# Value products of two units formed with 512 weight columns at a time, in one layer of a hybrid decoder

## The chip, the cores and the metric

The kernel runs on one core of a Trainium2 chip. The metric is the device time in microseconds (us) of that core; a time of the kernel is the median of its runs. TensorE multiplies matrices, VectorE and ScalarE work element by element, GpSimd does small jobs here, and SyncE's queue issues the transfers. A matrix product on TensorE is an instruction pair: a weight load brings the stationary operand into the array, and the matmul streams the moving operand through it into a PSUM bank. A bank holds 512 f32 values on each of 128 partitions.

## The reference, cut to what matters

```python
u = rmsnorm(h, norm_w[l])
proj = jnp.einsum('bsd,dc->bsc', u, w_in[l])            # 1024 tokens, 2048 -> 8200 columns
(ml_q, ml_k, ml_v, ml_o, ml_z, ml_i, ml_f,
 hg_q, hg_f, hg_i, hg_g) = jnp.split(proj, split_points, axis=-1)
qk = silu(causal_dwconv(concat([ml_q, ml_k]), conv_w[l], conv_b[l]))
h_a = mlstm_chunkwise(q_a, k_a, v_a, i_pre, f_pre)      # 4 heads, qk 128, value width 256
y_a = sigmoid(ml_o) * rmsnorm(h_a, ml_norm_w) * silu(ml_z)
h_b = hgrn2_chunkwise(hg_q, k_b, logf_b, hg_i)          # 8 heads, state 128 x 128
y_b = rmsnorm(h_b, hg_norm_w) * silu(hg_g)
h = h + einsum('bsc,cd->bsd', concat([y_a, y_b]), w_out[l])
gate = sigmoid(einsum('bsd,de->bse', rmsnorm(h, pe_norm_w[l]), w_pg[l]))
h = h + gate * einsum('bsr,rd->bsd', p[l], w_pe[l])
out = rmsnorm(h, final_norm_w)
```

The change concerns the two value columns sets, `ml_v` and `hg_i`: eight blocks of 256 columns, of which each product is (1024 x 2048) times (2048 x 256).

## The kernel before, in words

The 1024 tokens are worked on in two halves of 512. For each half the input is brought in transposed, 16 tiles `u` of 128 channels by 512 tokens, each as two parts (a rounded high part and the rest, low). Every weight is halved in the same way: `split` (L117) lets ScalarE write the high part (L118) and VectorE the rest (L119). A product then takes three matmuls, high by high, high by low, low by high (`mm3`, L245 to L248).

The combined projection is cut into 32 blocks `b` of 256 columns a half. Weights come as pieces of 512 KB, four for a block, in the order of the list `w_order` (L128 to L142). `next_piece` (L144) transfers one into `raw` and halves it into `hl`; both have three buffers, and a piece is asked for three pieces ahead (`AHEAD`).

Most blocks go through `proj_ch` (L250): the weights are stationary and the 512 tokens of the half move, into two PSUM banks `pj`. The value blocks go through `proj_tok` (L262): the activations are stationary, 128 tokens at a time, and the 256 weight columns move. Four banks `pt` are filled, one for each group of 128 tokens, and half of each is used. For a block that is 16 channels tiles x 4 token groups x 3 matmuls = 192 matmuls. The pool `pj` has four banks for both kinds.

A half has eight units, one after the other: four mLSTM heads (`mlstm_unit`, L345, blocks 4 hd to 4 hd + 3, the value block is the third) and four pairs of HGRN heads (`hgrn_unit`, L466, blocks 16 + 4 pr to 19 + 4 pr, the value block is the first). In the first head's value block eight gate columns ride along (264 columns). ScalarE reads the four banks of a value block into `vt` (L389, L476), scaled by each token's norm; `vt` has two buffers.

A unit's mixing follows its projections and runs beside the projections of the next unit: small products on TensorE with VectorE and ScalarE steps between them. For an HGRN unit I call this its chain. It starts with column sums (`cs_d`, `cs_s`, L518 and L519), goes through five levels (`pl`, L574, then a masked copy at L579 and two updates at L585 and L587), then states and outputs (`hkt`, `hpu`, `hpo`), a norm, and two transposes back (`hpt`, L644, then `hy`, L646). After both halves come the output projection (`po`), the gate projection (`pg`) and the last norm.

The order of the instructions on each engine is not the one in which the code is written. A scheduler places them from priorities and from its own costs when the program is built, so a change in one product moves the mixing steps between the products too. On the chip each engine then runs its list in that order and waits by semaphores.

Of the kernel before, what the change touches and what calls it, by code (L numbers as in the profile page):

```python
# [16 lines left out]
F32 = mybir.dt.float32  # L17
# [3 lines left out]
AF = mybir.ActivationFunctionType  # L21
# [3 lines left out]
P = 128  # L25
S = 1024
D = 2048
KT = D // P
HT = 512
NC = HT // P  # L30
# [4 lines left out]
BIG = 1e30  # L35
LEVELS = (4, 8, 16, 32, 64)
NMASK = 3 + len(LEVELS)
HOLD = 2
LATE = [f"bg1_3_{pc}" for pc in (1, 3, 5, 7)]

# [1 line left out]


@with_exitstack
def hybrid_layer(ctx: ExitStack, tc, x, xT, pT, w_blk, w_v0, w_out, w_pg, w_pe, vec, gb, fnw,
                 ident_in, causal_in, lmask_in, out):
    nc = tc.nc
    PS = bass.MemoryType.PSUM
# [14 lines left out]
    mix = mixctx.enter_context(tc.tile_pool(name="mix", bufs=1))  # L63

    def psj(name):
        return pj.tile([P, 512], F32, tag="pj", name=name)
# [10 lines left out]
    causal = const.tile([P, P], F32, name="causal")  # L77
    lmask = mix.tile([P, NMASK, 64], U32, name="lmask")
    gb_sb = const.tile([4, 2], F32, name="gb_sb")
# [48 lines left out]
    w_order, w_tiles = [], []  # L128
    for half in range(2):
        for b in range(32):  # L130
            for pc in range(4):
                src = w_v0 if b == 2 else w_blk[b]
                w_order.append((f"{half}_{b}_{pc}", src[:, pc * 4:(pc + 1) * 4, :]))
    for half in range(2):
# [31 lines left out]
    def load_piece(name):  # L166

        while len(w_tiles) < len(w_order) and (len(w_tiles) < AHEAD or w_order[len(w_tiles) - AHEAD][0] != name):
            next_piece()
        return dict(w_tiles[-AHEAD - 4:])[name]  # L170
# [74 lines left out]
    def mm3(ps, ah, al, bh, bl, first, last):  # L245
        nc.tensor.matmul(ps, lhsT=ah, rhs=bh, start=first, stop=False)  # L246
        nc.tensor.matmul(ps, lhsT=ah, rhs=bl, start=False, stop=False)  # L247
        nc.tensor.matmul(ps, lhsT=al, rhs=bh, start=False, stop=last)  # L248
# [13 lines left out]
    def proj_tok(half, us, b, n=256):  # L262

        ps = [psj(f"pt{half}_{b}_{i}") for i in range(NC)]
        for pc in range(4):
            hl = load_piece(f"{half}_{b}_{pc}")
            for kk in range(4):
                k = pc * 4 + kk
                sl = slice(kk * n, (kk + 1) * n)
                for t in range(NC):  # L270
                    ts = slice(t * P, (t + 1) * P)
                    mm3(ps[t][:, 0:n], us[k][:, 0, ts], us[k][:, 1, ts], hl[:, 0, sl], hl[:, 1, sl],
                        k == 0, k == KT - 1)
        return ps


    def gates(half, pv, rc):
# [68 lines left out]
    def mlstm_unit(half, us, hd, rs, gc):  # L346
        n = f"{half}_{hd}"
        b0 = hd * 4
# [4 lines left out]
        rc, rb = rs  # L353
# [22 lines left out]
        q, k = qk[:, 0], qk[:, 1]  # L376
# [5 lines left out]
            nc.vector.tensor_tensor(out=gate[:, i], in0=po[i], in1=rb, op=ALU.mult)  # L382
        nc.scalar.activation(out=gate, in_=gate, func=AF.Sigmoid)

        pv = proj_tok(half, us, b0 + 2, 264 if hd == 0 else 256)
        vt = mix.tile([P, NC, 257], F32, tag="vt", bufs=2, name=f"vt{n}")
        nc.vector.memset(vt[:, :, 256:257], 1.0)
        for t in range(NC):
            nc.scalar.activation(out=vt[:, t, 0:256], in_=pv[t][:, 0:256], func=AF.Copy, scale=rc[:, t:t + 1])  # L389
        if hd == 0:  # L390
            gc = gates(half, pv, rc)
        cols, rows = gc
# [75 lines left out]
    def hgrn_unit(half, us, pr, rs):  # L468
        rc, rb = rs
        b0 = 16 + pr * 4  # L470
        n = f"{half}_{pr}"
        H2 = 2 * NC
        pv = proj_tok(half, us, b0)
        vt = mix.tile([P, NC, 257], F32, tag="vt", bufs=2, name=f"hv{n}")
        for t in range(NC):
            nc.scalar.activation(out=vt[:, t, 0:256], in_=pv[t][:, 0:256], func=AF.Copy, scale=rc[:, t:t + 1])  # L476

        def v_of(i, c):
            return vt[:, c, i * P:(i + 1) * P]
# [3 lines left out]
        f = mix.tile([P, 2, HT + 3], F32, tag="raw", bufs=1, name=f"f{n}")  # L483
        f = f.rearrange("p a b -> p (a b)")[:, 0:2 * HT].rearrange("p (a b) -> p a b", b=HT)
        gate = mix.tile([P, 2, HT], F32, tag="gate", bufs=2, name=f"hgate{n}")
        for i in range(2):
            hd = pr * 2 + i
# [63 lines left out]
        for i in range(2):  # L551
            ps = col_sums(prod[:, i], f"s2{n}_{i}").rearrange("p (c b j t) -> p c b j t", c=NC, j=2, t=2)
            for j in range(2):
                nc.vector.copy_predicated(
                    out=at.rearrange("p c (b a s) -> p c b a s", a=2, s=2)[:, i * NC:(i + 1) * NC, :, 1, :],
# [11 lines left out]
        for li, s in enumerate(LEVELS):  # L567
# [10 lines left out]
            else:  # L578
                nc.vector.copy_predicated(  # L579
                    out=at.rearrange("p c (b two s) -> p c b two s", two=2, s=s)[0:M, :, :, 1, :],  # L580
# [15 lines left out]
        for i in range(2):  # L596
            hd = pr * 2 + i
# [40 lines left out]
        for i in range(2):  # L638
            hd = pr * 2 + i
# [12 lines left out]
    for half in range(2):  # L652
        us = prep_u(half)
        gc = None
        for hd in range(4):
            gc, rs = mlstm_unit(half, us, hd, rs, gc)
        nrs = prep_stats(1) if half == 0 else None
        if half == 1:
            mlctx.close()
            xh = ctx.enter_context(tc.tile_pool(name="xh", bufs=4, side="right", reuse_waits="tile"))  # L660
        for pr in range(4):
            hgrn_unit(half, us, pr, rs)
        rs = nrs
# [4 lines left out]
    for half in range(2):  # L668
# [14 lines left out]
        for cb in range(4):  # L683
            ps = [psj(f"po{half}_{cb}_{t}") for t in range(NC)]
            for pc in range(8):
                hl = load_piece(f"o{half}_{cb}_{pc}")
                for kk in range(2):
                    k = pc * 2 + kk
# [16 lines left out]
            for j in range(4):  # L705
                k = cb * 4 + j
# [15 lines left out]
        def gate_block(cb, ts_, pref):  # L722
# [13 lines left out]
            for t in ts_:  # L736
                parts = 2 if pref == "b" and t == NC - 1 else 1
                w = 512 // parts
                units += [(t, slice(i * w, (i + 1) * w), psj(f"pg{half}_{cb}_{t}_{i}")) for i in range(parts)]
            hold = HOLD if pref == "b" else 8  # L740
            hls = []
# [58 lines left out]
def _layout(inp):  # L800
    f = np.float32
    x = np.ascontiguousarray(np.asarray(inp["x"])[0])
    w = np.asarray(inp["w_in"])[0]
    cols = []
    for h in range(4):
        cols.append([(h * 128, 128), (512 + h * 128, 128)])
        cols.append([(2048 + h * 256, 256)])
        cols.append([(1024 + h * 256, 256)])
        cols.append([(3072 + h * 256, 256)])
    for p in range(4):  # L810
        q, fg, i, g = 4104 + p * 256, 5128 + p * 256, 6152 + p * 256, 7176 + p * 256
        cols.append([(i, 256)])
        cols.append([(q, 128), (fg, 128)])
        cols.append([(q + 128, 128), (fg + 128, 128)])
        cols.append([(g, 256)])
    v0 = np.empty((P, KT, 264), f)
    v0[:, :, 0:256] = w[:, 1024:1280].reshape(KT, P, 256).transpose(1, 0, 2)
    v0[:, :, 256:264] = w[:, 4096:4104].reshape(KT, P, 8).transpose(1, 0, 2)
    blk = np.empty((32, P, KT, 256), f)
    for b, cs in enumerate(cols):  # L820
        o = 0
        for c, n in cs:
            blk[b, :, :, o:o + n] = w[:, c:c + n].reshape(KT, P, n).transpose(1, 0, 2)
            o += n
    def blocks(m, kt):
        return np.ascontiguousarray(np.asarray(m)[0].reshape(kt, P, 4, 512).transpose(2, 1, 0, 3))

    vec = np.empty((P, V_END), f)
    vec[:, V_NORM:V_NORM + 16] = np.asarray(inp["norm_w"])[0].reshape(16, P).T
    vec[:, V_PEN:V_PEN + 16] = np.asarray(inp["pe_norm_w"])[0].reshape(16, P).T  # L830
    vec[:, V_MLN:V_MLN + 8] = np.asarray(inp["ml_norm_w"])[0].reshape(8, P).T
    vec[:, V_HGN:V_HGN + 8] = np.asarray(inp["hg_norm_w"])[0].reshape(8, P).T
    vec[:, V_LB:V_LB + 16] = np.asarray(inp["hg_lb"]).reshape(16, P).T
    vec[:, V_CW:V_CW + 32] = np.asarray(inp["conv_w"])[0].reshape(4, 8, P).transpose(2, 1, 0).reshape(P, 32)
    vec[:, V_CB:V_CB + 8] = np.asarray(inp["conv_b"])[0].reshape(8, P).T
    gb = np.stack([np.asarray(inp["ml_b_i"])[0], np.asarray(inp["ml_b_f"])[0]], axis=1)

    ident = np.eye(P, dtype=f)
    jj, tt = np.meshgrid(np.arange(P), np.arange(P), indexing="ij")
    causal = np.where(jj <= tt, 0.0, -BIG).astype(f)  # L840
    lm = np.zeros((P, NMASK, 64), np.uint32)
    j = np.arange(P)[:, None]
    c = np.arange(64)
    lm[:, 0] = j == 2 * c
    lm[:, 1] = j == c // 2 * 4
    lm[:, 2] = j == c // 2 * 4 + 1
    for li, s in enumerate(LEVELS):
        t = (c // s) * 2 * s + s + c % s
        lm[:, 3 + li] = (j // (2 * s) == t // (2 * s)) & ((j // s) % 2 == 0)
    return {  # L850
        "x": x, "xT": np.ascontiguousarray(x.T),
        "pT": np.ascontiguousarray(np.asarray(inp["p"])[0, 0].T.reshape(2, P, S).transpose(1, 0, 2)),
        "w_blk": blk, "w_v0": v0, "w_out": blocks(inp["w_out"], KT), "w_pg": blocks(inp["w_pg"], KT),
        "w_pe": blocks(inp["w_pe"], 2), "vec": vec, "gb": np.ascontiguousarray(gb),
        "fnw": np.ascontiguousarray(np.asarray(inp["final_norm_w"]).reshape(1, D)),
        "ident": ident, "causal": causal, "lmask": lm,
    }
# [16 lines left out]
```

## Time and profile before

| what | value |
|---|---|
| median of 3 runs | 2389.89 us (2389.16 to 4723.31) |
| the profiled execution, its own time | 2389.19 us |
| its span on the core | 2387.2 us |
| mean granted TensorE clock | 0.999 |
| TensorE busy | 2370.0 us, 99% of the span |
| VectorE, ScalarE busy | 1165.5 us (49%), 766.2 us (32%) |
| moved by DMA | 287.57 MB, mean 120 GB/s |

The span goes from the first to the last instruction; the profiled execution's own time is 1.99 us more. In the rows further down, a line such as `L247 PE MATMUL pt<-hl,u` names the line of the kernel, the engine, the operation, what is written and what is read. The busy time of TensorE counts a matmul from its start to its modelled end. Since matmuls are pipelined, one begins before the one ahead of it has ended, so the duration of one says little about its price; the distance from start to start does.

### The profile page before, as it was taken

The page shows a single profiled execution, that of the slowest core. Times are in us where ns is not written, and L with a number is a line of the kernel's source. Part 1 is how long each engine was busy: PE and PEld are TensorE (multiplying, and loading weights), DVE is VectorE, ACT ScalarE, POOL GpSimd, SP SyncE. Part 2 cuts the span into 40 slices and gives each one's busy share as a digit, 9 for nine tenths or more (in the row PEclk, how much of TensorE's full clock was granted, in tenths as well). Part 3 has the DMA queues.
Part 4 walks back from the last instruction along what each step waited for, and adds up shares of the span by engine and source line. Part 5 has one row for each costly group of instructions (what it writes and reads, how often), then busy time and mean ns, then how long its engine had stood idle before and what let it go on. Part 6 is the DMA issues. An engine that isn't in the chain of part 4 may idle for free.

```text
span 2387.2 us, 30855 instructions
## 1 busy us (share of the span) xinstructions
PE 2370.0 (99%) x12700; PEld 2043.5 (86%) x12700; DVE 1165.5 (49%) x1657; ACT 766.2 (32%) x1211; POOL 66.5 (3%) x96
## 2 busy tenths in 40 slices
PE   8999999999999999999999999999999999999998
PEld 7898889898888898988898898988888888888887
DVE  6655344455564847344346364565433444333336
ACT  6433232223222434223222222242422334332235
POOL 0000000000000000000000000000000000000000
PEclk9999999999999999999999999999999999999999
DMA  8433333323222523333332222244444446444346
GB/s 319 140 98 106 95 102 95 94 78 95 79 89 76 164 81 106 98 108 104 93 111 89 88 80 89 80 146 125 145 128 129 134 150 222 143 159 131 117 118 217
DMA packets 93461, 287.57 MB, mean 120 GB/s; under 512 B 10872, under 2 KB 11640, under 8 KB 93320
## 3 DMA queue, kind: packets, MB, share of 16 engines
q1 hardware_dynamic: 88200, 268.82, 36.3%
q0 software_dynamic: 5120, 16.78, 1.8%
q8 instruction: 99, 1.62, 0.3%
q14 instruction: 42, 0.34, 0.0%
HBM read 260.36 MB, written 25.20 MB: 120 GB/s over the span
## 4 chain that ended last, share of the span: by engine, by line
PE 98%; DMA 0%; issue 0%; DVE 0%; ACT 0%; SPq 0%; POOL 0%; POOLq 0%; ACTq 0%; DVEq 0%
PE pj L246 15%; PE pj L247 15%; PE pj L248 15%; PE pt L246 5%; PE pt L247 5%; PE pt L248 5%; PE po L246 5%; PE pg L247 5%; PE pg L248 5%; PE po L247 5%; PE po L248 5%; PE pg L246 5%; PE pl L574 2%; PE pe L246 1%; PE pe L248 1%; PE pe L247 1%
## 5 line engine op out<-in xcount | busy, mean ns | idle before, releaser
L246 PE MATMUL pj<-u,hl 128*128 128x512 f32 x1536 | 602.1, 395 | 6.5 <-ACT hl L118 5.8
L247 PE MATMUL pj<-u,hl 128*128 128x512 f32 x1536 | 602.5, 392 | 0.2 <-DVE u L234 0.2
L248 PE MATMUL pj<-u,hl 128*128 128x512 f32 x1536 | 600.2, 391 | 0.0
L118 ACT CAST hl<-raw 128x1024 fp32r<-128x1024 f32 (+2 forms) x259 | 269.0, 1039 | 832.9 <-PE pj L248 575.7
L119 DVE TENSOR_TENSOR hl<-raw,hl 128x1024 fp32r<-128x1024 f32 (+2 forms) x259 | 313.5, 1211 | 385.8 <-ACT hl L118 385.4
L246 PEld LDWEIGHTS pj<-u,hl 128*128 128x128 f32 x1536 | 288.7, 188 | 66.3 <-ACT hl L118 5.8
L248 PEld LDWEIGHTS pj<-u,hl 128*128 128x128 f32 x1536 | 288.7, 188 | 59.7 <-issue 0.2
L247 PEld LDWEIGHTS pj<-u,hl 128*128 128x128 f32 x1536 | 289.0, 188 | 59.2 <-DVE u L234 1.1
L246 PE MATMUL pt<-hl,u 128*128 128x256 f32 (+1 forms) x1024 | 290.5, 285 | 0.5 <-DVE raw L361 0.5
L247 PE MATMUL pt<-hl,u 128*128 128x256 f32 (+1 forms) x1024 | 290.1, 284 | 0.0
L248 PE MATMUL pt<-hl,u 128*128 128x256 f32 (+1 forms) x1024 | 289.8, 285 | 0.0
L246 PE MATMUL po<-hl_o,ys 128*128 128x512 f32 x512 | 200.4, 392 | 0.0
L247 PE MATMUL po<-hl_o,ys 128*128 128x512 f32 x512 | 200.2, 391 | 0.0
L248 PE MATMUL po<-hl_o,ys 128*128 128x512 f32 x512 | 199.4, 390 | 0.0
L246 PEld LDWEIGHTS pt<-hl,u 128*128 128x128 f32 x1024 | 195.4, 191 | 2.1 <-issue 1.1
L247 PEld LDWEIGHTS pt<-hl,u 128*128 128x128 f32 x1024 | 195.7, 191 | 1.2
L248 PEld LDWEIGHTS pt<-hl,u 128*128 128x128 f32 x1024 | 195.0, 191 | 0.9 <-issue 0.2
L246 PE MATMUL pg<-hl_g,hnt 128*128 128x512 f32 x448 | 174.9, 390 | 0.0
L247 PE MATMUL pg<-hl_g,hnt 128*128 128x512 f32 x448 | 174.5, 390 | 0.0
L248 PE MATMUL pg<-hl_g,hnt 128*128 128x512 f32 x448 | 174.3, 389 | 0.0
L119 DVE TENSOR_TENSOR hl_o<-raw_o,hl_o 128x1024 fp32r<-128x1024 f32 x64 | 78.4, 1225 | 157.9 <-ACT hl_o L118 157.9
L119 DVE TENSOR_TENSOR hl_g<-raw_g,hl_g 128x1024 fp32r<-128x1024 f32 x56 | 68.6, 1225 | 166.3 <-ACT hl_g L118 166.3
(264 smaller groups left out, 2640.7 us busy)
## 6 DMA issues: line engine op xcount, KB each, us to landing
raw<-in_w_blk_dram SPq DMA_DIRECT2D x247, 512.0 KB, 3.8
raw_o<-in_w_out_dram SPq DMA_DIRECT2D x64, 512.0 KB, 3.6
raw_g<-in_w_pg_dram SPq DMA_DIRECT2D x56, 512.0 KB, 3.6
yr<-y SPq DMA_DIRECT2D x32, 256.0 KB, 3.9
xr<-in_x_dram SPq DMA_DIRECT2D x32, 256.0 KB, 5.8
h<-ht POOLq DMA_DIRECT2D x32, 256.0 KB, 6.5
hr<-h SPq DMA_DIRECT2D x32, 256.0 KB, 3.7
out_dram<-h SPq DMA_DIRECT2D x32, 256.0 KB, 3.2
```

Of the source, the lines that this page charges most:

```text
L118: nc.scalar.copy(out=dst_hi, in_=src)
L119: nc.vector.tensor_tensor(out=dst_lo, in0=src, in1=dst_hi.bitcast(F32), op=ALU.subtract)
L246: nc.tensor.matmul(ps, lhsT=ah, rhs=bh, start=first, stop=False)
L247: nc.tensor.matmul(ps, lhsT=ah, rhs=bl, start=False, stop=False)
L248: nc.tensor.matmul(ps, lhsT=al, rhs=bh, start=False, stop=last)
L574: nc.tensor.matmul(pl[0:M, c * 64:(c + 1) * 64], lhsT=kf[:, c * P:c * P + M], rhs=qv[:, c * nb:(c + 1) * nb, 1, :], start=True, stop=True)
```

## The change

Six of the eight value blocks of a half are formed in pairs. `WIDE` names the first block of each pair: 10 with 14 (third and fourth mLSTM head), 16 with 20, 24 with 28 (HGRN units 0 and 1, 2 and 3). The weights of a pair lie side by side in a new input `w_vw`, 512 columns wide, and arrive in eight pieces of two channel tiles, still 512 KB each. `proj_tok` is called once with 512 moving columns and fills the four banks whole. ScalarE then reads each bank twice, into two `vt` tiles; the second waits in the list `vts` until its unit takes it, and for this `vt` has three buffers. Blocks 2 and 6 of each half stay as they were.

```diff
+WIDE = (10, 16, 24)
...
         for b in range(32):
+            if b in WIDE:
+                for pc in range(8):
+                    w_order.append((f"{half}_{b}_{pc}", w_vw[WIDE.index(b), :, pc * 2:(pc + 1) * 2, :]))
+                continue
             for pc in range(4):
+                if b - 4 in WIDE:
+                    continue
                 src = w_v0 if b == 2 else w_blk[b]
                 w_order.append((f"{half}_{b}_{pc}", src[:, pc * 4:(pc + 1) * 4, :]))
...
     def proj_tok(half, us, b, n=256):
 
         ps = [psj(f"pt{half}_{b}_{i}") for i in range(NC)]
-        for pc in range(4):
+        nk = 2 if n == 512 else 4
+        for pc in range(KT // nk):
             hl = load_piece(f"{half}_{b}_{pc}")
-            for kk in range(4):
-                k = pc * 4 + kk
+            for kk in range(nk):
+                k = pc * nk + kk
                 sl = slice(kk * n, (kk + 1) * n)
                 for t in range(NC):
                     ts = slice(t * P, (t + 1) * P)
                     mm3(ps[t][:, 0:n], us[k][:, 0, ts], us[k][:, 1, ts], hl[:, 0, sl], hl[:, 1, sl],
                         k == 0, k == KT - 1)
         return ps
+
+    vts = []
+
+    def values(half, us, b, rc, n):
+
+        if b - 4 in WIDE:
+            return None
+        wide = b in WIDE
+        pv = proj_tok(half, us, b, 512 if wide else n)
+        for i in range(2 if wide else 1):
+            vt = mix.tile([P, NC, 257], F32, tag="vt", bufs=3, name=f"vt{half}_{b}_{i}")
+            for t in range(NC):
+                nc.scalar.activation(out=vt[:, t, 0:256], in_=pv[t][:, i * 256:(i + 1) * 256], func=AF.Copy,
+                                     scale=rc[:, t:t + 1])
+            vts.append(vt)
+        return pv
...
-        pv = proj_tok(half, us, b0 + 2, 264 if hd == 0 else 256)
-        vt = mix.tile([P, NC, 257], F32, tag="vt", bufs=2, name=f"vt{n}")
+        pv = values(half, us, b0 + 2, rc, 264 if hd == 0 else 256)
+        vt = vts.pop(0)
         nc.vector.memset(vt[:, :, 256:257], 1.0)
-        for t in range(NC):
-            nc.scalar.activation(out=vt[:, t, 0:256], in_=pv[t][:, 0:256], func=AF.Copy, scale=rc[:, t:t + 1])
...
-        pv = proj_tok(half, us, b0)
-        vt = mix.tile([P, NC, 257], F32, tag="vt", bufs=2, name=f"hv{n}")
-        for t in range(NC):
-            nc.scalar.activation(out=vt[:, t, 0:256], in_=pv[t][:, 0:256], func=AF.Copy, scale=rc[:, t:t + 1])
+        values(half, us, b0, rc, 256)
+        vt = vts.pop(0)
...
+    vw = np.empty((3, P, KT, 512), f)
+    for i, b in enumerate(WIDE):
+        vw[i, :, :, 0:256] = blk[b]
+        vw[i, :, :, 256:512] = blk[b + 4]
```

In the order of the instructions this shows at two places. In both, a name such as `pt_24_0` is bank 0 of block 24, and `hl_24_2` is a weight piece of that block. The first is ScalarE at the end of block 24 in the first half. Before:

```order
L118 CAST hl_25_1_5026<-raw_25_1_5025 128x1024
L476 ACTIVATE hv_2_5078<-pt_24_0_4862,rx_394 128x256
L476 ACTIVATE hv_2_5078<-pt_24_1_4863,rx_394 128x256
L476 ACTIVATE hv_2_5078<-pt_24_2_4864,rx_394 128x256
L476 ACTIVATE hv_2_5078<-pt_24_3_4865,rx_394 128x256
L118 CAST hl_25_2_5090<-raw_25_2_5089 128x1024
```

Now:

```order
L119 CAST hl_25_1_4678<-raw_25_1_4677 128x1024
L295 ACTIVATE vt_24_0_4706<-pt_24_0_4470,rx_394 128x256
L295 ACTIVATE vt_24_1_4711<-pt_24_0_4470,rx_394 128x256
L295 ACTIVATE vt_24_0_4706<-pt_24_1_4471,rx_394 128x256
L295 ACTIVATE vt_24_1_4711<-pt_24_1_4471,rx_394 128x256
L295 ACTIVATE vt_24_0_4706<-pt_24_2_4472,rx_394 128x256
L295 ACTIVATE vt_24_1_4711<-pt_24_2_4472,rx_394 128x256
L295 ACTIVATE vt_24_0_4706<-pt_24_3_4473,rx_394 128x256
L295 ACTIVATE vt_24_1_4711<-pt_24_3_4473,rx_394 128x256
L119 CAST hl_25_2_4723<-raw_25_2_4722 128x1024
```

Eight reads stand where four stood, bank by bank, between the same two weight casts.

The second place is TensorE from the end of the first HGRN unit's chain (`hpt_0`) to the start of the second one's (`cs_d_1`). Before, where 111 matmuls of blocks 22 and 23 stand between them:

```order
L644 MATMUL hpt_0_0_4036<-ident,hn_0_4034 128x128 x4
L644 MATMUL hpt_0_1_4045<-ident,hn_0_4034 128x128 x4
L246 MATMUL pj_22_1_4404<-u_13_238,hl_22_3_4435 128x512
...
L248 MATMUL pj_23_1_4529<-u_15_246,hl_23_3_4560 128x512
L518 MATMUL cs_d_1_0_4657<-hl_d_1_0_4654,ones_r 128x512
L519 MATMUL cs_d_1_0_4657<-hl_d_1_0_4654,ones_r 128x512
```

Now, where 37 matmuls of block 24 stand between them:

```order
L664 MATMUL hpt_0_0_3865<-ident,hn_0_3863 128x128 x4
L664 MATMUL hpt_0_1_3874<-ident,hn_0_3863 128x128 x4
L253 MATMUL pt_24_1_4471<-hl_24_0_4197,u_1_180 128x512
...
L253 MATMUL pt_24_3_4473<-hl_24_1_4226,u_3_188 128x512
L538 MATMUL cs_d_1_0_4265<-hl_d_1_0_4262,ones_r 128x512
L254 MATMUL pt_24_3_4473<-hl_24_1_4226,u_3_188 128x512
L538 MATMUL cs_d_1_1_4272<-hl_d_1_1_4269,ones_r 128x512
```

The first chain now ends inside block 24 and the second begins 37 matmuls later; before, a whole block without mixing lay between them. In all the program has 1152 TensorE matmuls fewer: 2304 with 256 columns go, 1152 with 512 come.

## Rows read from the trace of the kernel before

**Rows 1.** The page, parts 1, 2 and 4: busy shares, granted clock, chain.
```profile
PE 2370.0 (99%) x12700; PEld 2043.5 (86%) x12700; DVE 1165.5 (49%) x1657; ACT 766.2 (32%) x1211; POOL 66.5 (3%) x96
...
PEclk9999999999999999999999999999999999999999
...
PE 98%; DMA 0%; issue 0%; DVE 0%; ACT 0%; SPq 0%; POOL 0%; POOLq 0%; ACTq 0%; DVEq 0%
```

**Rows 2.** What TensorE waited for, longest and last of five rows: us, times, longest.
```profile
PE pj L246 <- ACT hl L118: 5.8, 1, 5.8
...
PE pj L247 <- DVE u L234: 0.2, 1, 0.2
```

**Rows 3.** TensorE by line and shape: busy us, mean ns; idle before.
```profile
L247 PE MATMUL pj<-u,hl 128*128 128x512 f32 x1536 | 602.5, 392 | 0.2 <-DVE u L234 0.2
...
L246 PE MATMUL pt<-hl,u 128*128 128x256 f32 x896 | 254.2, 285 | 0.0
...
L246 PE MATMUL po<-hl_o,ys 128*128 128x512 f32 x512 | 200.4, 392 | 0.0
```

**Rows 4.** TensorE in time, a value product: start us, us; 33 starts apart.
```profile
166.02 0.28 PE L247 MATMUL pt<-hl,u 128*128 128x256 f32 x1
...
169.98 0.28 PE L247 MATMUL pt<-hl,u 128*128 128x256 f32 x1
```

**Rows 5.** TensorE in time, a product with 512 moving activation columns; 14 starts apart.
```profile
99.69 0.39 PE L248 MATMUL pj<-u,hl 128*128 128x512 f32 x1
...
102.86 0.39 PE L247 MATMUL pj<-u,hl 128*128 128x512 f32 x1
```

**Rows 6.** TensorE in time, the output projection (512 moving weight columns); 9 apart.
```profile
1699.76 0.39 PE L246 MATMUL po<-hl_o,ys 128*128 128x512 f32 x1
...
1701.80 0.39 PE L246 MATMUL po<-hl_o,ys 128*128 128x512 f32 x1
```

**Rows 7.** Two stretches: us, busy (instructions) of each engine, granted clock, DMA share, GB/s.
```profile
165.90:169.90 4.00, 4.00 (x36) 4.00 (x35) 0.00 (x0) 0.92 (x1) 0.00 (x0) 1.00 0.42 131
99.70:109.70 10.00, 10.00 (x46) 8.29 (x45) 9.61 (x15) 6.36 (x6) 0.00 (x0) 1.00 0.26 88
```

**Rows 8.** Readers of a value product: ns min/median/max of one, then four in time.
```profile
L476 ACT ACTIVATE hv<-pt,rx x32: 467/476/482, 417.1 to 1530.0; 128x256 f32<-128x256 f32 x32
...
417.12 1.57 ACT L476 ACTIVATE hv<-pt,rx 128x256 f32<-128x256 f32 x4 [3.63 <-PE pt L248]
```

**Rows 9.** The page, parts 5 and 6: halving a weight piece, and its transfer.
```profile
L118 ACT CAST hl<-raw 128x1024 fp32r<-128x1024 f32 (+2 forms) x259 | 269.0, 1039 | 832.9 <-PE pj L248 575.7
L119 DVE TENSOR_TENSOR hl<-raw,hl 128x1024 fp32r<-128x1024 f32 (+2 forms) x259 | 313.5, 1211 | 385.8 <-ACT hl L118 385.4
...
raw<-in_w_blk_dram SPq DMA_DIRECT2D x247, 512.0 KB, 3.8
```

**Rows 10.** TensorE in time, two level products that follow each other.
```profile
503.88 1.80 PE L574 MATMUL pl<-hq,kg 128*120 128x64 f32 x16
...
510.12 1.69 PE L574 MATMUL pl<-hq,kg 128*112 128x64 f32 x16
```

**Rows 11.** VectorE in time between these two; in brackets idle time before.
```profile
505.72 0.72 DVE L579 COPY_PREDICATED at<-lmask,pl 120x512 f32<-120x512 uint32 x1 [2.33 <-PE pl L574]
...
506.93 0.69 DVE L587 TENSOR_TENSOR kg<-kg,tot 128x512 f32<-128x512 f32 x1
```

**Rows 12.** TensorE in time, end of one unit's chain and start of the next.
```profile
562.50 1.03 PE L644 MATMUL hpt<-ident,hn 128*128 128x128 f32 x8
...
588.54 0.39 PE L518 MATMUL cs_d<-hl_d,ones_r 128*128 128x512 f32 x1
```

**Rows 13.** VectorE in time between these two.
```profile
563.13 1.41 DVE L646 SCALAR_TENSOR_TENSOR hy<-hpt,vec_sb,hgate 128x512 f32<-128x512 f32 x2 [0.18 <-PE hpt L644]
...
570.67 1.22 DVE L525 TENSOR_TENSOR pd<-hq,kg 128x1024 f32<-128x1024 f32 x1
...
573.47 0.68 DVE L119 TENSOR_TENSOR hl_d<-pd,hl_d 128x512 fp32r<-128x512 f32 x1
```

More of the change, by code (lines that the diff above doesn't have):

```diff
@@ L44, in hybrid_layer @@
 @with_exitstack
-def hybrid_layer(ctx: ExitStack, tc, x, xT, pT, w_blk, w_v0, w_out, w_pg, w_pe, vec, gb, fnw,
+def hybrid_layer(ctx: ExitStack, tc, x, xT, pT, w_blk, w_v0, w_vw, w_out, w_pg, w_pe, vec, gb, fnw,
                  ident_in, causal_in, lmask_in, out):
@@ L852, in _layout @@
         "pT": np.ascontiguousarray(np.asarray(inp["p"])[0, 0].T.reshape(2, P, S).transpose(1, 0, 2)),
-        "w_blk": blk, "w_v0": v0, "w_out": blocks(inp["w_out"], KT), "w_pg": blocks(inp["w_pg"], KT),
+        "w_blk": blk, "w_v0": v0, "w_vw": vw, "w_out": blocks(inp["w_out"], KT), "w_pg": blocks(inp["w_pg"], KT),
         "w_pe": blocks(inp["w_pe"], 2), "vec": vec, "gb": np.ascontiguousarray(gb),
```

## The prediction

> **What bounds the kernel now.** I read the shares of the page first, then the chain of waits, then TensorE's own waits, and only then single instructions in time. The page says that TensorE is busy for 2370.0 us of a span of 2387.2 us, at a granted clock that stays at the top of its two levels (2.4 GHz) in all 40 slices, and the chain that ended last lies on TensorE for 98% [rows 1]. Its waits are five in all, from 5.8 us at the start down to 0.2 us, 8.2 us together [rows 2]. So VectorE (49%) and ScalarE (32%) are hidden, and a change counts by what it does to the row of matmuls on TensorE, and by whether it brings new waits there.
>
> The next view misleads if it is read quickly. By line and shape a value matmul with 256 columns lasts 285 ns and one with 512 lasts 392 ns [rows 3]. These durations overlap: the three `pj` rows, 1536 matmuls each at some 392 ns, would add up to 1805 us, and matmuls of the other kinds would not fit in what is left. What a matmul costs is the distance between starts. In a value product 33 starts take 3.96 us, 0.1200 us each [rows 4]. With 512 moving columns 14 starts take 3.17 us, 0.2264 us [rows 5]. Both stretches have a clock of 1.00 and TensorE busy throughout [rows 7]. The output projection is of the very form that the change makes, activations stationary and 512 weight columns moving: 9 starts take 2.04 us, 0.2267 us [rows 6]. I take 0.2267.
>
> **The change part by part.**
>
> *The products.* A half loses six blocks of 192 matmuls with 256 columns and gets three of 192 with 512. Over both halves 2 x 6 x 192 = 2304 matmuls go, at 0.1200 us: 276.5 us. 2 x 3 x 192 = 1152 come, at 0.2267 us: 261.2 us. The difference is 15.3 us. Seen per pair, two narrow matmuls take 0.2400 us and a wide one 0.2267 us, so 13.3 ns are saved 1152 times: twice the columns cost less than twice the time, because some 13 ns of each matmul do not depend on its columns. All of it is on the path, since TensorE is never idle here. With 0.2264 us it would be 15.7 us.
>
> A rule of the Trainium skill would make it less. TensorE: Matmul & The Clock Gate, section Back-to-back issue gap, gives N/2.4 + 2.5 ns from start to start at the high clock, thus a fixed part of 2.5 ns; 1152 times that, an estimate from this page, would be 2.9 us and the time 2386. The trace does not agree: the formula gives 109 and 216 ns where the rows have 120.0 and 226.7, so I stay with the rows.
>
> *The weights.* The pieces are 512 KB as before and as many: four and four become eight. A piece of a value block lasted 48 x 0.1200 = 5.76 us on TensorE and now lasts 24 x 0.2267 = 5.44 us. That is what every piece of the other blocks lasts already (24 matmuls with 512 columns), and those run without a wait. A piece needs 3.8 us to land and 1.04 + 1.21 us for the two halves [rows 9], and is asked for three pieces ahead, so I cost this at nothing. Without that cover it would cost at most 5.44 us a place.
>
> *Reading the banks.* Each wide product has eight reads instead of four. One takes 476 ns, but four in a row take 1.57 us [rows 8], so eight take 3.1 us. ScalarE has the room (32% busy). They stand ahead of a weight cast, `hl_25_2` in the order shown, which now waits some 1.6 us longer. TensorE needs that piece only two pieces after the end of the block, 10.9 us later, so the cast and VectorE's half (2.3 us) still fit. The bank itself is the tighter point, since the next product wants banks 0 and 1. In the new order ScalarE reads bank by bank, so a bank is free after two reads, 0.8 us, and TensorE finishes the four banks three matmuls (0.7 us) apart. I take 0. Below nothing is excluded, since no read goes away. The upper bound is that TensorE waits for all eight each time: 6 x 3.1 = 18.8 us.
>
> *The third buffer.* It takes away no wait that the trace shows, for none of the five is for a `vt` [rows 2]. The second half of a pair only lies longer. Nothing either way.
>
> *The mixing that moves.* This is the part with the real doubt. The second unit of a pair has three products of 96 x 0.2267 = 21.8 us left, where it had a value product of 192 x 0.1200 = 23.0 us beside them. The scheduler answers by letting the chains of the two units of a pair follow each other. Inside a chain the distances do not shrink. Between two levels 28 matmuls of 512 columns stand in the new order, 6.3 us, where 38 of 256 (4.6 us) stood. In the trace the next level's product starts at 510.12 us, after one that began at 503.88 us [rows 10], and what it needs is ready at 506.93 + 0.69 = 507.62 us, 2.5 us early [rows 11]. So there is more room than before.
>
> The place where room goes is between chains. Before, 26.0 us passed from the last transposes of the first unit (562.50 us) to the first column sums of the second (588.54 us) [rows 12]. Now it is eight transposes, 0.8 us (the next matmul follows them 0.79 us later), and 37 x 0.2267 = 8.4 us: 9.2 us. In that time VectorE must do `hy` (1.41 us), the product `pd` (1.22 us) and one half of its split (0.68 us) [rows 13], a gate product of the same size as `pd` (1.22 us) and one weight half (1.21 us [rows 9]): 5.7 us, with a ScalarE cast of half a weight piece between them, below 1.04 us. That is 6.8 of 9.2 us. It fits, with 2.4 us to spare, and I take 0 here too. There are four such places, the second and fourth HGRN unit of each half. The upper bound is that each column sum starts as late after the transposes as before: 4 x (26.0 - 9.2) = 67 us. Below, the small waits of before could vanish with the new order, at most the 2.4 us of the four short ones.
>
> *The sum.* 2389.19 us for the profiled execution, less 15.3 us, plus 0: 2373.9 us. I put down 2374. That execution lies 0.7 us below the median of the runs, which changes nothing at this size.
>
> **The rivals.**
>
> *New waits eat part of it.* At the end of the six wide products, or at one of the dense places of VectorE, TensorE stands 1 to 3 us. For it: the margin of 2.4 us between the chains is narrow, and the first head of the second half puts its convolution steps on VectorE at the same time. Against it: the waits are nearly none today, and the reads are ordered by bank. Six waits of 0.8 us and four of 1.5 us make 11 us: 2385; with all six full waits 2393. Chance 0.15.
>
> *The chain of the second unit is late (slower).* Place: the column sums of the second and fourth unit of each half. Mechanism: VectorE, in order, still has the last steps of the first chain, the gate and the weight halves ahead of `pd`, and TensorE, whose list is fixed, stands at `cs_d`. It begins to cost when the work between needs over 9.2 us. The gain is gone at 9.2 + 15.3/4 = 13.0 us, and the kernel is slower by over 2% from some 25 us on. At its full price the time is 2374 + 67 = 2441. For it: VectorE's steps are in order, and one late step delays all behind it. Against it: the rows give 6.8 us of work, and TensorE has the rest of block 24 to run only after the column sums. Chance 0.05, mostly between 2389 and 2410.
>
> *The change saves no fixed part.* If a wide value matmul took exactly what two narrow ones take (0.2400 us), the time would stay at 2389. For it: no value product with 512 columns is in the trace. Against it: the output projection is the same form and has 0.2267 us [rows 6]. Chance 0.03.
>
> *The durations are the price.* If 285 and 392 ns [rows 3] were what a matmul costs, 1152 x (2 x 285 - 392) ns = 205 us would be saved: 2184. Against it: the starts in rows 4 to 6. Chance 0.01. The same page of the Trainium skill also names 131 ns for sustained matmuls with 512 columns; no stretch here comes near it, the rows having 227 ns.
>
> **How the numbers follow.** My forecast, 2371 to 2379, has 0.75; the likeliest time is 2374. The waits have 0.15, the late chain 0.05, no fixed part 0.03, the durations 0.01, and 0.01 is left. The range of 8 in 10 goes from 2370 (15.7 us saved, and the small waits gone) to 2386, which takes in most of the case with new waits. A difference of 2% (48 us) is about what a measurement of this kernel tells from no change. The forecast, the waits and the missing fixed part all lie within it. Only the late chain near its full price is slower by more: 0.03 with what I may have missed. Only the durations are faster by more: 0.01. Within 2%: 0.96.
>
> **What would show it.** In the new profile the wide value matmuls start 0.227 us apart; the count of value matmuls is 1152 with 512, 384 with 256 and 384 with 264 columns; TensorE's busy time falls by some 15 us while its waits stay under 12 us. Weight piece and bank waits would show as `pj` waiting for a `vt` or for `hl`. A late chain would show as `cs_d` or `pl` waiting for VectorE, several us each. The prediction is wrong if the starts lie 0.240 us apart, or if TensorE's waits grow by over 10 us.

## The result, and the profile after

The changed kernel takes 2373.71 us in the median (2372.51 to 2374.66, 6 runs), the kernel before 2388.97 us beside it: ratio 0.9936, interval 0.9923 to 0.9950. That is 15.3 us or 0.6% less, against a forecast of 2374; the whole interval lies below 1. One of the six runs of the kernel before took 4723.31 us; without it their median is 2388.78 us and the difference 15.1 us. The profiled execution, the fastest of the six, took 2372.51 us with a span of 2370.5 us.

The page of the changed kernel: busy us, share of the span and instructions of each engine; the granted clock in 40 slices; the chain that ended last.

```profile
PE 2355.8 (99%) x11548; PEld 1984.1 (84%) x11548; DVE 1170.9 (49%) x1657; ACT 765.8 (32%) x1211; POOL 66.3 (3%) x96
...
PEclk9999999999999999999999999999999999999999
...
PE 99%; DMA 0%; DVE 0%; SPq 0%; ACT 0%; issue 0%; ACTq 0%; POOLq 0%
```

Against [rows 1] TensorE has 1152 instructions and 14.2 us fewer. Clock and shares stand as they were, and the chain is still TensorE's.

What TensorE waited for, the whole list: us in total, times, longest.

```profile
PE pj L253 <- ACT hl L119: 5.3, 1, 5.3
PE pt L253 <- DVE raw L385: 0.5, 1, 0.5
```

Five waits with 8.2 us [rows 2] have become two with 5.8 us. No wide product waits for a weight, no product behind one waits for a bank, and TensorE waits for VectorE in no chain.

TensorE by line and shape, one of the three new `pt` rows (busy us, mean ns), and then two starts of one wide product, 14 apart.

```profile
L253 PE MATMUL pt<-hl,u 128*128 128x512 f32 x384 | 150.4, 392 | 0.0
```

```profile
585.67 0.39 PE L253 MATMUL pt<-hl,u 128*128 128x512 f32 x1
...
588.85 0.39 PE L255 MATMUL pt<-hl,u 128*128 128x512 f32 x1
```

3.18 us / 14 = 0.227 us from start to start, as in the output projection [rows 6]. The duration, 392 ns, again says nothing about the price. With 0.227 us the products save 2304 x 0.1200 - 1152 x 0.2270 = 15.0 us. The span fell by 16.7 us: these 15.0, the 2.4 us of waits that are gone, less 0.7 us that no view shows by itself. Between the medians, where every execution counts, it is 15.3 us.

The place between two chains that answers to [rows 12, 13], TensorE first, then VectorE, then ScalarE.

```profile
584.11 1.03 PE L664 MATMUL hpt<-ident,hn 128*128 128x128 f32 x8
...
593.38 0.39 PE L538 MATMUL cs_d<-hl_d,ones_r 128*128 128x512 f32 x1
...
594.74 0.39 PE L539 MATMUL cs_d<-hl_d,ones_r 128*128 128x512 f32 x1
```

```profile
584.49 1.22 DVE L523 TENSOR_TENSOR hgate<-hgate,hsg 128x1024 f32<-128x1024 f32 x1
585.62 1.40 DVE L666 SCALAR_TENSOR_TENSOR hy<-hpt,vec_sb,hgate 128x512 f32<-128x512 f32 x2
586.94 1.21 DVE L545 TENSOR_TENSOR pd<-hq,kg 128x1024 f32<-128x1024 f32 x1
...
589.33 1.28 DVE L120 TENSOR_TENSOR hl_d<-pd,hl_d 128x512 fp32r<-128x512 f32 x2
```

```profile
588.19 1.14 ACT L119 CAST hl_d<-pd 128x512 fp32r<-128x512 f32 x2 [3.92 <-DVE pd L545]
```

From `hpt` to `cs_d` it is 593.38 - 584.11 = 9.27 us; the forecast had 9.2. The column sums of L538 need ScalarE's casts: both are ready at 588.19 + 1.14 = 589.33 us, 4.05 us ahead of the first column sum (counted from the first of the two casts some 4.6 us, the figure in expectations further down). Those of L539 need VectorE's halves, ready at 590.61 us and first used at 594.74 us, 4.13 us later. So 2.4 us of slack were forecast, and there are over 4.

### The profile page after: what moved, and what is told of

Its sections match the earlier page's. It is cut to its first block, busy times and chain, and to the rows that moved or that the text cites. A ratio compares the mean times of both kernels' runs of the same rounds, so it can differ in the third digit from the quotient of the medians.

```text
span 2370.5 us, 28577 instructions
## 1 busy us (share of the span) xinstructions
PE 2355.8 (99%) x11548; PEld 1984.1 (84%) x11548; DVE 1170.9 (49%) x1657; ACT 765.8 (32%) x1211; POOL 66.3 (3%) x96
## 4 chain that ended last, share of the span: by engine, by line
PE 99%; DMA 0%; DVE 0%; SPq 0%; ACT 0%; issue 0%; ACTq 0%; POOLq 0%
PE pj L254 15%; PE pj L253 15%; PE pj L255 15%; PE pt L253 5%; PE pt L255 5%; PE pt L254 5%; PE po L253 5%; PE pg L253 5%; PE po L255 5%; PE pg L254 5%; PE po L254 5%; PE pg L255 5%; PE pl L594 2%; PE pe L255 1%; PE pe L254 1%; PE pe L253 1%
## 5 line engine op out<-in xcount | busy, mean ns | idle before, releaser
L254 PE MATMUL pt<-hl,u 128*128 128x512 f32 (+2 forms) x640 | 223.7, 350 | 0.0
L253 PE MATMUL pt<-hl,u 128*128 128x512 f32 (+2 forms) x640 | 222.9, 349 | 0.5 <-DVE raw L385 0.5
L255 PE MATMUL pt<-hl,u 128*128 128x512 f32 (+2 forms) x640 | 221.9, 348 | 0.0
L253 PEld LDWEIGHTS pt<-hl,u 128*128 128x128 f32 x640 | 120.6, 189 | 15.7 <-issue 0.8
L254 PEld LDWEIGHTS pt<-hl,u 128*128 128x128 f32 x640 | 120.8, 189 | 14.9 <-issue 0.2
L255 PEld LDWEIGHTS pt<-hl,u 128*128 128x128 f32 x640 | 120.5, 189 | 15.0 <-issue 0.2
```

## The experiments

All were timed against the kernel before on the same chip (2389.13 us for the first four, 2389.09 us for the others). "The changed kernel" is the one with 2373.71 us. It was timed with the result and not again beside them, so differences of one or two microseconds from it rest on the waits in the traces more than on the times. My theory: the gain is a fixed part of each matmul that does not depend on its moving columns, and nothing else moves the time. The rivals: the gain comes from the new order of the work, or from the reads and buffers.

### The wide product issued as two halves

```diff
-                    mm3(ps[t][:, 0:n], us[k][:, 0, ts], us[k][:, 1, ts], hl[:, 0, sl], hl[:, 1, sl],
-                        k == 0, k == KT - 1)
+                    ah, al = us[k][:, 0, ts], us[k][:, 1, ts]
+                    for j in range(2):
+                        c = slice(j * 256, (j + 1) * 256)
+                        s2 = slice(kk * 512 + j * 256, kk * 512 + (j + 1) * 256)
+                        bh, bl = hl[:, 0, s2], hl[:, 1, s2]
...
+                        nc.tensor.matmul(ps[t][:, c], lhsT=ah, rhs=bh, start=False, stop=False)
+                        nc.tensor.matmul(ps[t][:, c], lhsT=ah, rhs=bl, start=False, stop=False)
+                        nc.tensor.matmul(ps[t][:, c], lhsT=al, rhs=bh, start=False, stop=last)
```

> The changed kernel with each wide value matmul issued as two with 256 columns into the two halves of the same bank; weight pieces, banks, the double reads and the third buffer stay, and the mixing stays behind the pairs. Theory (a fixed part of 13.3 ns in each matmul, 1152 fewer of them): the 15.3 us come back, so about 2389 us, 2386 to 2392, and starts 0.120 us apart in blocks 10, 16 and 24. Rival (the gain comes from the moved mixing, the fewer small waits or the weight pieces): all that is kept, so 2374 to 2377 us.

Measured: 2387.6 us (2387.06 to 2389.58), ratio 0.9994 (0.9985 to 1.0003). Its page, its waits, and two starts of a value product, 36 apart:

```profile
PE 2370.3 (99%) x12700; PEld 2044.8 (86%) x12700; DVE 1170.0 (49%) x1657; ACT 767.9 (32%) x1211; POOL 66.5 (3%) x96
```

```profile
PE pj L253 <- ACT hl L119: 5.8, 1, 5.8
PE pt L253 <- DVE raw L408: 0.5, 1, 0.5
```

```profile
591.38 0.28 PE L303 MATMUL pt<-hl,u 128*128 128x256 f32 x1
...
595.70 0.28 PE L303 MATMUL pt<-hl,u 128*128 128x256 f32 x1
```

With the weights, reads, buffers and small waits of the changed kernel, but matmuls of 256 columns at 4.32 / 36 = 0.1200 us, 13.9 us of the gain are gone. TensorE's busy time is back at 2370.3 us, that of [rows 1]. What is left, 1.5 us, cannot be told from no change (the interval takes in 1); the waits here are 1.9 us shorter than in [rows 2]. The order built for this version is not the same to the last instruction, but the chains of a pair follow each other as in the changed kernel: 7.3 to 9.5 us from `hpt` to `cs_d` at the four places. So the gain is the width of the matmul and not the order around it.

### One pair, two pairs

```diff
-WIDE = (10, 16, 24)
+WIDE = (10,)
```

For two pairs the line reads `WIDE = (16, 24)`. What was expected of one pair, and then of two:

> Only the mLSTM pair (blocks 10 and 14) is formed at 512 columns, one pair a half. Theory: a third of the matmuls saved, 384 x 13.3 ns = 5.1 us, so 2383.9 us, 2382.5 to 2385.5. Rival (the gain sits in the HGRN units, where the chains were moved): 2389 us. Rival (the gain sits in the mLSTM pair alone): 2374 us.

> Only the two HGRN pairs (16 with 20, 24 with 28) are formed at 512 columns, two pairs a half. Theory: two thirds, 768 x 13.3 ns = 10.2 us, so 2378.7 us, 2377 to 2380.5. Rival (the gain sits in the HGRN units): 2374 us. Rival (it sits in the mLSTM pair): 2389 us.

Measured: 2385.87 us (2384.17 to 2388.0), ratio 0.9986 (0.9978 to 0.9995), for one pair, just above the range that was expected; 2377.86 us (2377.63 to 2378.37), ratio 0.9954 (0.9941 to 0.9966), for two, inside it. Two pairs save 11.3 us where 10.2 follow from the working. One pair saves 3.3 us where 5.1 do; its interval, 1.2 to 5.3 us, still takes in 5.1. A wait that the changed kernel has not is longer here than before. It stands below as it was before, then as it is here, with VectorE just ahead of it here:

```profile
PE prow L286 <- DVE gp L281: 1.0, 1, 1.0
```

```profile
PE prow L310 <- DVE gp L305: 2.7, 1, 2.7
```

```profile
881.64 0.48 DVE L353 MEMSET stk<- 68x512 f32 x1 [4.86 <-DMA y<-hy]
882.05 0.49 DVE L305 TENSOR_SCALAR gp<-pt,rx 128x8 f32<-128x8 f32 x4
```

The gate columns `gp` that TensorE waits for stand on VectorE behind a memset, and VectorE stood for 4.86 us before that memset, until the transfer of an earlier result (`y<-hy`) had ended. In the profiled execution this makes 1.7 us of the 1.8 us that are missing. In the changed kernel's order `gp` comes before the memset, and TensorE does not wait. Neither pair holds the gain by itself, as the rivals have it: each gives a part, and the one pair does so with the HGRN chains where they were before (26.0 us from `hpt` to `cs_d`). The gain grows with the pairs, and beside each size stand one or two microseconds of small waits that come and go with the order.

### Two buffers for the values

```diff
-            vt = mix.tile([P, NC, 257], F32, tag="vt", bufs=3, name=f"vt{half}_{b}_{i}")
+            vt = mix.tile([P, NC, 257], F32, tag="vt", bufs=2, name=f"vt{half}_{b}_{i}")
```

> All three pairs, but with two buffers for the value tiles instead of three. In the order built for it, the rest of the second HGRN unit's chain (last level, states, outputs) now stands between the end of block 24 and block 25 with no product to fill it, once a half. Theory: the third buffer is what keeps the gain. Without it TensorE waits some 10 to 15 us in each half at that place, so 2394 to 2404 us, slower than both. Rival (the buffer does not matter, since none of the waits of before was for it): 2374 us.

Measured: 2393.07 us (2388.95 to 2395.39), ratio 1.0014 (1.0005 to 1.0023). The whole gain is lost; the time is a little below the 2394 to 2404 that were expected. Its longest waits, then a place where they come, as busy us (instructions) of TensorE, its weight loads, VectorE, ScalarE and GpSimd, granted clock, DMA share and GB/s, and then TensorE there:

```profile
PE pl L594 <- DVE kg L607: 4.1, 2, 2.1
PE hkt L621 <- DVE kg L607: 4.1, 2, 2.1
PE hpu L625 <- ACT hkh L622: 2.7, 4, 0.7
```

```profile
634.00:636.00 2.00, 2.00 (x20) 1.74 (x18) 0.00 (x0) 1.74 (x3) 0.00 (x0) 1.00 0.35 141
636.00:638.00 2.00, 0.02 (x1) 0.00 (x0) 1.94 (x4) 0.14 (x1) 0.00 (x0) 1.00 0.00 0
...
640.00:645.00 5.00, 3.04 (x13) 2.67 (x14) 1.14 (x2) 0.58 (x1) 0.00 (x0) 0.50 0.34 105
645.00:650.00 5.00, 4.32 (x20) 3.92 (x19) 2.47 (x8) 0.59 (x1) 0.00 (x0) 0.50 0.01 3
650.00:655.00 5.00, 4.54 (x32) 4.00 (x30) 0.20 (x1) 3.78 (x18) 0.00 (x0) 0.99 0.00 0
```

```profile
638.10 1.12 PE L594 MATMUL pl<-hq,kg 128*64 128x64 f32 x16 [2.07 <-DVE kg L607]
641.28 1.09 PE L621 MATMUL hkt<-ident,kg 128*128 128x128 f32 x4 [2.07 <-DVE kg L607]
643.04 2.07 PE L625 MATMUL hpu<-vt,hkh 128*128 128x128 f32 x8 [0.68 <-ACT hkh L622]
```

ScalarE, the reads of the second half of block 24:

```profile
652.53 1.56 ACT L295 ACTIVATE vt<-pt,rx 128x256 f32<-128x256 f32 x4
```

The second half of block 24 leaves its banks only when the chain that still reads the older `vt` has ended on TensorE, at 652 us, and the next block needs these banks. So the steps of that chain follow one another on TensorE with no product between them, and each VectorE and ScalarE step shows as a wait. The waits make 19.0 us in all, 13.2 more than in the changed kernel, while its span is 21.7 us longer. 11.7 us of them stand at this place and its like in the second half, so 5.9 us a half where 10 to 15 were expected. Most of the other 8.5 us is the clock, which was not in the expectation: after TensorE had stood, it was granted 0.50 (1.2 GHz) for about 10 us here, and 0.50 to 0.59 for 15 us at the other place. TensorE was busy for 19.0 us in these stretches; at full clock the same work would have taken about 9 us less, an estimate from these shares.

### The reads in two passes

```diff
-                nc.scalar.activation(out=vt[:, t, 0:256], in_=pv[t][:, i * 256:(i + 1) * 256], func=AF.Copy,
-                                     scale=rc[:, t:t + 1])
+                if i == 0:
+                    rd = nc.scalar.activation(out=vt[:, t, 0:256], in_=pv[t][:, 0:256], func=AF.Copy,
+                                              scale=rc[:, t:t + 1])
+                else:
+                    with tc.issue_after(rd.ins):
+                        nc.scalar.activation(out=vt[:, t, 0:256], in_=pv[t][:, 256:512], func=AF.Copy,
+                                             scale=rc[:, t:t + 1])
```

> As the changed kernel, but ScalarE reads the four banks of a wide product for the first unit, then all four again for the second, in place of both reads of a bank together. Theory: bank 0 ends about 1.9 us before the product and was free 0.8 us after its end; now it is free only after five reads, some 1.0 us after the product's end, so TensorE waits up to 1.0 us at each of the six wide products where no mixing product stands between: 0 to 6 us, 2374 to 2380, likeliest 2377, and the wait shows as pj or pt waiting for a ScalarE read of pt. Rival (the order of the reads does not matter, banks are never the bound): 2374 and no such wait. Rival (a bank is handed over only when all eight reads are done): 6 x 3.1 = 18.8 us, 2392, and then the same wait should be in the changed kernel.

Measured: 2375.6 us (2374.57 to 2376.01), ratio 0.9942 (0.9928 to 0.9957): 1.9 us more than the changed kernel. ScalarE and TensorE at the end of block 16 in the changed kernel, then the wait here, and TensorE and ScalarE at the same end here:

```profile
433.57 3.02 ACT L295 ACTIVATE vt<-pt,rx 128x256 f32<-128x256 f32 x8 [2.35 <-PE pt L255]
```

```profile
435.41 0.39 PE L253 MATMUL pj<-u,hl 128*128 128x512 f32 x1
```

```profile
PE pj L253 <- ACT vt L300: 1.9, 2, 0.9
```

```profile
436.79 0.50 PE L253 MATMUL pj<-u,hl 128*128 128x512 f32 x1 [0.93 <-ACT vt L300]
```

```profile
436.27 1.56 ACT L300 ACTIVATE vt<-pt,rx 128x256 f32<-128x256 f32 x4
```

In the changed kernel the eight reads begin 1.84 us before the next product, and bank 0 is free after two of them. Here the next product waits for the fifth read. It waits only twice, behind block 16 in each half; the list shows no such wait at the other four wide products. Behind block 10 the mLSTM products `psc` and `pkt` stand on TensorE at this point (1.25 us to the next `pj`), and behind block 24 a level product (1.30 us), and these cover it, in the changed kernel as here. So reading by bank is worth about 1 us at the two places without cover.

### More VectorE work between the chains

```diff
+        if pr % 2 == 1:
+            for _ in range(12):
+                nc.vector.tensor_tensor(out=prod, in0=q, in1=kG, op=ALU.add)
```

The other version has `range(4)`. What was expected with four additions, and then with twelve:

> As the changed kernel, with four more VectorE additions of 1.22 us (4.9 us) ahead of the first product pd of the second and fourth HGRN unit of each half, the four places where the chains of a pair now follow each other. Theory (slack there is 4.6 us, and the program's order puts the column sums some 30 products later for it): hidden, 2374, 2372 to 2376. Rival (the late chain: TensorE stands at the column sums for what goes over the 4.6 us of slack): 4 x 0.3 us with the order unchanged, so under 2 us, and a wait of cs_d for VectorE in the list.

> As the changed kernel, with twelve more VectorE additions of 1.22 us (14.6 us) at the same four places, 58.6 us of VectorE in all. Theory: the order puts the column sums about 90 products (20 us) later, the wide product covers them, and the time stays at 2374, 2372 to 2378. Rival (the late chain): the delay goes over the 4.6 us of slack by 10 us at each of four places, 2414, and TensorE waits for VectorE at cs_d by about 10 us each.

Measured: 2375.49 us (2375.37 to 2376.55), ratio 0.9944 (0.9929 to 0.9958), with four additions; 2382.13 us (2381.59 to 2382.73), ratio 0.9970 (0.9959 to 0.9982), with twelve. The first lies inside the range that was expected; neither theory has the second. In neither does TensorE wait at a `cs_d`; with twelve, the long wait beside that for the first weight (5.3 us) is elsewhere. The wait, then TensorE, VectorE and two stretches (columns as above) at that place:

```profile
PE hpt L667 <- DVE hn L663: 5.2, 1, 5.2
```

```profile
1698.23 1.97 PE L667 MATMUL hpt<-ident,hn 128*128 128x128 f32 x8 [5.20 <-DVE hn L663]
```

```profile
1697.49 1.29 DVE L663 TENSOR_TENSOR hn<-hpo,hr 128x512 f32<-128x512 f32 x2 [1.85 <-POOL hr L125]
```

```profile
1695.00:1699.00 4.00, 0.77 (x4) 0.77 (x5) 1.93 (x4) 1.21 (x4) 1.66 (x1) 0.56 0.56 178
1699.00:1703.00 4.00, 4.00 (x22) 3.82 (x20) 2.88 (x5) 0.69 (x1) 1.14 (x2) 0.58 0.36 128
```

At three of the four places 14.6 us of added work cost next to nothing; the list has one wait of 0.3 us there. By the starts in its trace `cs_d` comes there 29.0 to 30.8 us after `hpt` instead of 8.1 to 9.5, and the products between hide the delay. At the fourth, the last unit of the second half, the column sums are put off in the same way (30.1 us), but the chain then ends later: its last transposes go from 1681.3 to 1698.2 us. There only the start of the output projection lies beside it, and 5.2 us of the chain's own length come to light, of the 8.4 us that the time is longer than the changed kernel's; in the two stretches shown the granted clock is 0.56 and 0.58 of full speed, thus mostly at 1.2 GHz. With four additions the last transposes go to 1688.1 us, and four waits, 2.2 us together, stand in the output projection that the changed kernel has not; the median is 1.8 us higher. The longest of them:

```profile
PE pht L732 <- DVE hnt L736: 0.8, 1, 0.8
```

My theory was right that the column sums have cover and wrong that the whole chain has. The rival was wrong on the place, and its 2414 with it. Both versions were given an order that puts the column sums later, so what the slack of 4 us is worth with the order unchanged is not shown.

### The spacing of matmuls by themselves

```diff
+    for j in range(N):
+        nc.tensor.matmul(t[:, 0:256], lhsT=st(ar, j, P), rhs=mv(ar, 256), start=j == 0, stop=j == N - 1)
```

`N` is 96; `st` gives one of eight stationary blocks in turn, `mv` the moving columns. This is the run with 256 columns; the others differ in columns and type.

> This kernel computes nothing of the layer: it issues runs of 96 matmuls of one form back to back, each run on its own line, after 300 matmuls that warm the clock: rounded f32 (the form of the layer's products) with 512, 384 and 256 moving columns; the same with 64 stationary columns in place of 128; 256 columns with the same stationary block each time; then bf16 with 512 and 256, and plain f32 with 256 and 512. Theory: each matmul costs its columns at the clock's rate, plus a fixed part of 13.3 ns that does not depend on them: 226.7, 173.3 and 120.0 ns from start to start for 512, 384 and 256, and plain f32 double the columns' part with the same or a smaller fixed part. Rival one (the Trainium skill, TensorE: Matmul & The Clock Gate, Back-to-back issue gap): the spacing is N/2.4 + 2.5 ns and what the layer shows above that comes from something else in it: 215.8, 162.5 and 109.2 ns. Rival two: the fixed part is the load of the stationary block, so that it falls with 64 stationary columns (to about 6.7 ns: 220 and 113 ns) or goes when the block stays the same.

TensorE in this kernel, stretches within a run of one form: start, us, form, count. A stretch of n matmuls has n - 1 spacings and one duration at its end. It is one execution; the granted clock is 1.00 in all these stretches.

```profile
94.70 6.05 PE L51 MATMUL r<-ar 128*128 128x512 f32 x26
...
111.72 6.23 PE L55 MATMUL r<-ar 128*128 128x384 f32 x35
...
123.83 6.16 PE L59 MATMUL r<-ar 128*128 128x256 f32 x50
...
146.63 5.92 PE L63 MATMUL r512m<-ar 128*64 128x512 f32 x25
...
157.72 6.17 PE L67 MATMUL r256m<-ar 128*64 128x256 f32 x53
...
169.76 6.16 PE L71 MATMUL r256same<-ar 128*128 128x256 f32 x50
...
191.71 5.34 PE L75 MATMUL b<-ab 128*128 128x512 bf16 x24
...
204.83 3.11 PE L79 MATMUL b<-ab 128*128 128x256 bf16 x27
...
244.78 5.13 PE L83 MATMUL f<-raw 128*128 128x256 f32 x23
...
250.16 70.22 PE L87 MATMUL f<-raw 128*128 128x512 f32 x163 [0.26 <-ACT keep L36]
```

The weight loads of the run with the same stationary block each time: 96 loads, 192 ns each.

```profile
L71 PEld LDWEIGHTS r256same<-ar 128*128 128x128 f32 x96 | 11.6, 192 | 0.5 <-ACT keep L36 0.5
```

Taking off one duration (0.390, 0.336, 0.284, 0.393, 0.277, 0.284, 0.379, 0.273, 0.380 and 0.593 us by form), the spacings are 226, 173 and 120 ns for rounded f32 with 512, 384 and 256 columns; 230 and 113 with 64 stationary columns; 120 with the stationary block always the same; 216 and 109 in bf16. In plain f32 each matmul shows as two records, 192 for 96; the records are 216 ns apart with 256 columns and 430 with 512.

The three sizes lie on one line, 0.417 ns a column and 13.3 ns besides: the theory. The first rival, the rule of the Trainium skill (TensorE: Matmul & The Clock Gate, Back-to-back issue gap), fits bf16 to the nanosecond, 215.8 and 109.2, but not the rounded f32 of the layer. The second rival is right in one row and wrong in one. With 64 stationary columns 7 ns go at 256 moving columns, as it has it; at 512 nothing goes, and 4 ns are added. The row with the same block does not test it, since the block was loaded for every matmul all the same. What the 13.3 ns are stays open; that they do not depend on the moving columns is shown for 128 stationary columns.

The theory was wrong on plain f32. Its columns cost four times as much as those of rounded f32 and not twice (two records, each at 0.836 ns a column); the fixed part is smaller, 2 ns a record.

## Why the prediction was right, point by point

- **The products** carried the result. 0.2267 us was taken from the output projection and 0.227 was found; 15.3 us was the term, 15.0 us follows from the spacing. The two-halves version shows that the gain goes with the width, and the probe that the fixed part is the matmul form's own. The rule of the Trainium skill (TensorE: Matmul & The Clock Gate, Back-to-back issue gap) would have given 2386 here, an estimate from its figure. The trace and the probe do not agree with it for rounded f32: they have 227 and 226 ns with 512 columns, and the rule 216.
- **The weights at nothing**: right, no wide product waits for a weight.
- **The banks at nothing**: right. Behind block 16 it is for the reason given, the reading by bank: in another order these two places cost 0.9 us each. Behind blocks 10 and 24 a mixing product covers the reads, which the prediction did not count on. The upper bound of 18.8 us was far off, because at four places no wait shows in either order.
- **The third buffer, "nothing either way"**: right as a price, too weak as a statement. It removes no wait of before, but it is a condition of the gain: without it the change is 3.9 us slower than the kernel before it on that chip.
- **The moved mixing at nothing**: right, 9.27 us for 9.2. The slack is over 4 us and not 2.4, since the weight half that I counted after `hpt` ends while `hpt` runs, the gate product starts beside it, and the first column sums need ScalarE's casts alone. The bound of 67 us supposed that the column sums need the room they had before. They do not: they got 8.1 to 9.5 us in the changed kernel, and TensorE waits at none of them.
- **The small waits**: in the profiled execution they fell by 2.4 us, the end of the range and not the sum. This is luck. Only 1.0 us of it, at the gate rows, is the new order; one pair alone made this same wait 1.7 us longer. The other 1.4 us lie in the first 30 us, ahead of any wide product, and waits for `u` like the two that are gone there are back in six of the seven other versions of the layer.
- **The range**: 2370 as its lower end is 1 us under its own terms, 2389.19 - 15.7 - 2.4 = 2371.1 us. And 2% is far more than the least that a measurement of this kernel can tell: the interval of the result is 0.14% wide to either side.
- **The rivals**: new waits did not come, though they do with one pair alone or a buffer less. The late chain exists, but at the last unit's end and not at the column sums, and only with work added.

## What to carry to other kernels

Where TensorE never waits, price a change of matmul shape by the distance between starts of that very operand type, taken from a row where the new shape already runs; the durations and a rule for another type give other answers. A buffer that removes no wait today may still be what lets the new order stand, so ask what products would be left on TensorE beside a waiting chain without it. A chain's slack in the middle of a program says little about its end: the last unit has the least work beside it.

## What the runs showed that was not expected

- In two versions a short stand of TensorE was paid for twice. In the two-buffer version the granted clock fell to 0.50 during the second of two waits of 2.1 us and stayed there for about 10 us; in the version with twelve additions it was 0.56 in the stretch with the wait of 5.2 us and 0.58 in the 4 us behind it.
- Matmuls of rounded f32 are spaced by 13.3 ns more than their columns take, in bf16 by 2.5 ns (216 ns for 512 columns). With 64 stationary columns the excess is 7 ns at 256 moving columns and 17 ns at 512. No run explains either.
